# Block sums staged earlier, a branch result kept on chip and gates fetched a job ahead in a Fourier–Hyena encoder layer

## The chip, the cores and the metric

The kernel runs on one core of one Trainium2 chip. The metric is the device time of one execution in microseconds (us); the lower the better. All data are fp32. TensorE (PE) multiplies, VectorE (DVE), ScalarE (ACT) and GpSimd (POOL) do elementwise work, and transfers are issued from the queues of SyncE (SP) and GpSimd.

## The reference

Two sequences of 1024 rows and 1024 channels go through one encoder layer with two branches:

```
xn = rmsnorm(x, g_pre);  p = xn @ w_in        # columns: fv, fg, hv (3x), hg, mg (2x)
y_f = (fft2(fv).real * silu(fg)) @ w_fourier_out
v, x1, x2 = split(short_conv(hv))             # width-3 depthwise convolution
z = x1 * long_conv(v, k0);  z = x2 * long_conv(z, k1)
y_h = (z * silu(hg)) @ w_hyena_out
g_f, g_h = split(sigmoid(mg + b_merge))
out = x + rmsnorm((g_f * y_f + g_h * y_h) @ w_out, g_post)
```

The long convolutions' filters come from a small network and are normalized. "F" below is g_f * y_f, "H" is g_h * y_h.

## The kernel before

Matrices are held transposed, channels on partitions, in tiles of 128 channels by 1024 positions. Precision is kept by splitting each fp32 operand into a high part (a cast on ACT, line 171) and a low part (a subtraction, line 181), and multiplying high·high, high·low and low·high. So a loaded tile must pass ACT and then DVE or GpSimd before PE can use it.

The program has four parts in order of time. First come the Fourier transforms of both sequences (`phase_fourier`). Then 16 filter spectra are made, with projections of w_in as PE's filler (`spill_gate`: a projection whose result goes to DRAM as `d_g`, optionally multiplied by the Fourier result `d_fz`). Then the convolutions (`branches`), 16 steps for sequence 0 and 16 for sequence 1, again with projections; their results go to `d_sh`. Twelve more projections of sequence 1 (`PLAIN`, tiles `wr`, `wh`, `wl`) fill the end of this part. The fourth part, `phase_blocks`, is where most of the edit lies.

`phase_blocks` runs 34 jobs. Each job makes two output tiles of 128 channels by 1024 positions as a 2x2 block product in seven instead of eight block multiplications (Strassen–Winograd). A job's weights (`prepare`, tile `wraw`, its block sums `wsum`) are prepared a job or two ahead. The right operand is shared by all jobs of a kind: four plain blocks (`room`, tiles `b`) and four block sums (`sum_of`, tiles `tl`/`th`). There are six operands. Operand 0 (x of sequence 1) serves ten "x" jobs, which make the rest of the projections; operands 1 to 4 serve four jobs each (F of sequence 0, H of 0, F of 1, H of 1); operand 5, the weight w_out, serves the last eight "o" jobs. Where the operand changes, here called a turn, 7 MB of new blocks and sums must be loaded and split while PE goes from one job to the next.

The block sums of operands 1 to 5 are computed in this same part by `staged` (lines 1027 to 1039): during jobs, SP loads four blocks into `draw`, GpSimd forms four sums into `dsum` with three instructions and writes them to `d_t`; for w_out it also copies the plain blocks to `d_wo`. There are 20 such calls of 1 MB in and 1 MB out.

Each job drains four 128x512 results (`out`, lines 1090 to 1122), in the order of (tile, half) (0,0), (1,1), (0,1), (1,0). PE's accumulators are read by ACT into `u` and `m` (`kept`, line 1080), and DVE combines a second accumulator with them into `gt` (three buffers). An x job then applies SiLU on ACT, multiplies by a factor `fz` loaded for this result, and stores to `d_g`. An F or H job loads the merge gate `fz` (line 1114), takes its sigmoid on ACT (line 1115) and multiplies on DVE. F is stored to `d_m` (line 1122); H is added onto it by an accumulating transfer from GpSimd's queue (line 1120). The loads of `fz` are issued where the result is drained.

The order on each engine is set by a scheduler that plays the program through its own timeline. `tc.issue_after` holds a piece back until an instruction has been placed. Memory pools that open later reuse the space of closed ones, and wait for those tiles.

Of the kernel before, what the change touches and what calls it, by code (L numbers as in the profile page):

```python
# [16 lines left out]
P = 128  # L17
D = 1024
# [143 lines left out]
class K:  # L162
# [34 lines left out]
    def setup(self, ctx):  # L197
        tc, nc, a = self.tc, self.nc, self.a
        self.cp = cp = ctx.enter_context(tc.tile_pool(name="cp", bufs=1))
        self.ps = ctx.enter_context(tc.tile_pool(name="ps", bufs=2, space=bass.MemoryType.PSUM))  # L200
        self.dr = ctx.enter_context(tc.tile_pool(name="dr", bufs=1, space=bass.MemoryType.DRAM))

        def ld(name, shape, src, eng=nc.sync):
            t = cp.tile(shape, F32, name=name)
            eng.dma_start(t, src)
            return t
        self.ident = ld("ident", [P, P], a["c_id"], nc.gpsimd)
        self.gpre = ld("gpre", [P, 8], a["g_pre"], nc.gpsimd)
# [20 lines left out]
        self.d_wo = [dt(f"d_wo{k}", [P, D]) for k in range(8)]  # L229
        self.d_sh = [[dt(f"d_sh{b}_{k}", [P, L]) for k in range(8)] for b in range(NB)]  # L230
# [559 lines left out]
    def conv_back(self, n, ct, B, ws):  # L790
# [3 lines left out]
        for g, pairs in GROUPS:  # L794
# [3 lines left out]
            nc.sync.dma_start(kt.rearrange("p a b -> p (a b)"), self.d_k[n][ct][:, o:o + 8 * P])  # L798
# [98 lines left out]

    def branches(self, nb, nct, ws):
# [10 lines left out]
        plain = list(self.PLAIN)  # L909
        Z, X = {}, {}  # L910
# [21 lines left out]
        for i, (b, n, c) in enumerate(steps):  # L932
# [33 lines left out]
    def phase_blocks(self):  # L966
# [6 lines left out]
        jobs = [("x", s, c) for c in range(0, 8, 2) for s in (0, 4, 5, 6) if (s, c) not in self.PLAIN]  # L973
        for q in range(4):
            jobs += [("fh"[q % 2], q // 2, c) for c in range(0, 8, 2)]
        jobs += [("o", u, t) for u in range(4) for t in (0, 2)]
# [3 lines left out]
        def source(q):  # L980
            d = (self.d_g[0][0], self.d_sh[0], self.d_g[1][0], self.d_g[1][4], self.d_wo)[q - 1]
            return lambda k: d[k]
        with ExitStack() as es:
# [5 lines left out]
            def prepare(i):  # L989
# [3 lines left out]
                for j in range(2):  # L993
                    out = r[:, 2 * j:2 * j + 2].rearrange("p a b -> p (a b)")
                    if kind == "o":
                        nc.gpsimd.dma_start(out.rearrange("p (k c) -> p k c", k=8), self.d_m[x][:, :, P * (c + j):P * (c + j) + P])
                    else:
                        nc.gpsimd.dma_start(out, a["w_in"][x, c + j] if kind == "x" else a[f"w_{kind}o"][c + j])
                s = gw.tile([P, 4, 512], F32, tag="sum", name="wsum", bufs=1)
# [9 lines left out]
                self.add(eng, s[:, 0:2], r[:, 2].unsqueeze(1).to_broadcast([P, 2, 512]), r[:, 3::-3])  # L1009
                self.add(eng, s[:, 2], s[:, 0], r[:, 0])  # L1010
                parts("s2", gw, ("s2h", "s2l"), s[:, 2], 1)
                h, l = [gw.tile([P, 2, 4, P], F32R, tag=t, name=t, bufs=1) for t in ("s13h", "s13l")]
                f = lambda t: t.rearrange("p s a b -> p s (a b)")
                self.split(f(h), f(l), s[:, 0:2], "dve", "act")
                A["s1"], A["s3"] = (h[:, 0], l[:, 0]), (h[:, 1], l[:, 1])
                self.add(eng, s[:, 3], s[:, 2], r[:, 1])
                parts("s4", gw, ("s4h", "s4l"), s[:, 3], 1)
# [9 lines left out]
            def staged(q, k):  # L1027

                src = source(q)
                r = ga.tile([P, 4, 512], F32, tag="draw", name="draw", bufs=1)  # L1030
                for i in range(2):
                    nc.sync.dma_start(f2(r[:, 2 * i:2 * i + 2]), src(k + 4 * i) if q < 5 else a["w_out"][(k + 4 * i) * P:(k + 4 * i + 1) * P])
                    if q == 5:
                        nc.gpsimd.dma_start(src(k + 4 * i), f2(r[:, 2 * i:2 * i + 2]))
                s = ga.tile([P, 4, 512], F32, tag="dsum", name="dsum", bufs=1)
                self.sub("pool", s[:, 0::2], r[:, 0:2], r[:, 1::2])
                self.sub("pool", s[:, 1], s[:, 2], r[:, 0])
                self.add("pool", s[:, 3], s[:, 1], r[:, 2])
                nc.gpsimd.dma_start(self.d_t[q][:, k], s)

            def room(q, i, n):

                out = []
                for k in range(4):
                    t = xp.tile([P, 2, 512], F32R, tag=f"x{'hl'[i - n]}{k + 4 * n}", name=f"b{i}{n}{k}", bufs=1)
                    nc.sync.dma_start(t[:, 1].bitcast(F32), source(q)(k + 4 * i)[:, 512 * n:512 * n + 512])
# [18 lines left out]
            for k in range(4):  # L1065
# [3 lines left out]
                s = (ga, gw)[k % 2].tile([P, 4, 512], F32, tag=("dsum", "sum")[k % 2], name="xsum", bufs=1)  # L1069
                self.sub("dve", s[:, 0::2], r[:, 0:2], r[:, 1::2])  # L1070
                self.sub("dve", s[:, 1], s[:, 2], r[:, 0])
                self.add("dve", s[:, 3], s[:, 1], r[:, 2])
                for j in (1, 2, 0, 3):
                    self.split(T[j][0][:, k], T[j][1][:, k], s[:, j], "dve", "act")
# [14 lines left out]

            def out(i, j, n, p, q, op):  # L1090
# [4 lines left out]
                c += j  # L1095
                s = slice(512 * n, 512 * n + 512)
                t = wp.tile([P, 512], F32, tag="gt", name="gt", bufs=3)
                f = None
                if kind != "x" or x in (0, 4):
                    f = gw.tile([P, 512], F32, tag="f", name="fz", bufs=3)  # L1100
                if kind == "x":
                    if f is not None:
                        nc.sync.dma_start(f, (self.d_sh if x else self.d_fz)[1][c][:, s])
                    if q is not None:
                        self.tt("dve", t, p, q, op)
# [6 lines left out]
                    return  # L1112
                h = kind == "h"
                nc.sync.dma_start(f, self.d_g[x][6 if h else 5][c][:, s])
                nc.scalar.activation(f, f, AF.Sigmoid, bias=self.bm[:, 8 * h + c:8 * h + c + 1])
                if q is not None:
                    self.tt("dve", t, p, q, op)
                self.mul("dve", t, p if q is None else t, f)
                if h:
                    nc.gpsimd.dma_start(self.d_m[2 * x + n][:, c], t, accum_op=ADD)  # L1120
                else:
                    nc.sync.dma_start(self.d_m[2 * x + n][:, c], t)

            pa, pb, m1 = first(A)
            for i, job in enumerate(jobs):
                end = i + 1 == len(jobs)
                turn = not end and operand[i + 1] != operand[i]
                q = operand[min(i + 1, len(jobs) - 1)]
                if operand[i] == 5 and operand[i - 1] != 5:
                    st.close()  # L1130
# [41 lines left out]
                for p, k in {1: (1, 0), 2: (1, 1), 3: (1, 2), 4: (1, 3), 5: (2, 0), 6: (2, 1), 7: (2, 2), 8: (2, 3)}.items() if i < nx else ():  # L1172
                    if p == i:
                        staged(*k)
                if nx <= i < nx + 12:
                    staged(3 + (i - nx) // 4, (i - nx) % 4)

    def open_rows(self, op, jobs):
        nc, a = self.nc, self.a
        self.op, self.jobs = op, jobs  # L1180
        self.gp = op.tile([P, D], F32, name="gp")
# [3 lines left out]
    def open_row(self, i):  # L1185
# [3 lines left out]
        row = [512 * half + P * (t + j) for j in range(2)]  # L1189
# [110 lines left out]
```

## Time and profile before

| | |
|---|---|
| median of 3 runs | 2526.48 us (2525.7 to 2534.88) |
| the profiled execution | 2530.01 us |
| span in the profile | 2528.2 us |
| PE busy | 2398.2 us, 95% |
| DVE busy | 2083.5 us, 82% |
| ACT busy | 1128.3 us, 45% |
| GpSimd busy | 695.8 us, 28% |
| mean granted TensorE clock | 0.981 |

Busy times are shares of the span from the first to the last instruction. "Idle before" names what ended an engine's wait. "Granted clock" is the share of full speed at which TensorE was allowed to run; a PE that is busy at half clock still counts as busy. The last part (`phase_blocks`) starts its first product at about 1765 us.

### The profile page before, as it was taken

How to read it: one execution, taken by the hardware profiler on the slowest of the kernel's cores; microseconds unless marked ns; L12 is line 12 of the kernel's file. 1: busy time of each engine (PE TensorE's matmuls, PEld its weight loads, DVE VectorE, ACT ScalarE, POOL GpSimd, SP SyncE). 2: the span in 40 equal slices, each digit the busy share in tenths (PEclk: the TensorE clock that was granted, in tenths of full speed). 3: DMA queues.
4: the chain of work that ended last, by engine and by line, in shares of the span. 5: the costliest groups of instructions: out<-in, count | busy, mean ns of one | idle time of the engine just before them, and what ended most of it. 6: DMA issues, size and time to landing. Idle time of an engine off the chain costs nothing.

```text
span 2528.2 us, 36972 instructions
## 1 busy us (share of the span) xinstructions
PE 2398.2 (95%) x13004; PEld 2069.9 (82%) x13004; DVE 2083.5 (82%) x3696; ACT 1128.3 (45%) x2068; POOL 695.8 (28%) x588
## 2 busy tenths in 40 slices
PE   6999999999989999999999999999897988899898
PEld 6998888888878888888888888887786777677786
DVE  7786788888788999998989999876666887766887
ACT  6546666666643333333222223323343544444543
POOL 0331222211233434430000001113443555424221
PEclk9999999999999999999999999999999999899999
DMA  7636555554555545545434444437677888967654
GB/s 267 203 106 219 196 168 159 162 165 152 175 179 179 184 158 174 160 150 200 142 126 140 136 142 137 144 112 245 232 283 253 298 309 273 314 224 201 196 175 134
DMA packets 228594, 478.65 MB, mean 189 GB/s; under 512 B 23526, under 2 KB 70855, under 8 KB 225464
## 3 DMA queue, kind: packets, MB, share of 16 engines
q1 hardware_dynamic: 198876, 365.85, 44.3%
q0 software_dynamic: 29344, 110.42, 13.0%
q8 instruction: 102, 1.67, 0.3%
q14 instruction: 84, 0.69, 0.1%
q10 hardware_dynamic: 188, 0.02, 0.0%
HBM read 308.42 MB, written 167.77 MB: 188 GB/s over the span
## 4 chain that ended last, share of the span: by engine, by line
PE 36%; DMA 8%; DVE 5%; issue 3%; ACT 2%; POOL 1%; SPq 0%; DVEq 0%; ACTq 0%; POOLq 0%
PE pg L194 14%; PE pin L194 14%; PE pT L194 4%; PE pX L194 4%; DMA fz<-d_g 2%; DMA tl<-d_t 2%; DVE gt L181 1%; DVE tl L181 1%; DMA draw<-d_sh 1%; DMA xraw<-d_x 1%; DMA d_g<-gt 1%; DMA wraw<-in_w_in 1%; PE tph L786 1%; DMA b<-d_g 1%; DVE b L181 1%
## 5 line engine op out<-in xcount | busy, mean ns | idle before, releaser
L194 PE MATMUL pin<-xh,wh 128*128 128x512 f32 x1472 | 578.2, 394 | 3.6 <-DVE v L177 1.8
L194 PE MATMUL pin<-xh,wl 128*128 128x512 f32 x1472 | 577.0, 393 | 2.5 <-POOL wl L181 2.5
L194 PE MATMUL pin<-xl,wh 128*128 128x512 f32 x1472 | 578.4, 393 | 0.0
L181 POOL TENSOR_TENSOR wl<-wr,wh 128x512 fp32r<-128x512 f32 x136 | 252.5, 1857 | 1158.9 <-ACT wh L171 1142.9
L194 PEld LDWEIGHTS pin<-xh,wh 128*128 128x128 f32 x1472 | 278.3, 189 | 54.9 <-DVE v L177 2.0
L194 PEld LDWEIGHTS pin<-xh,wl 128*128 128x128 f32 x1472 | 278.3, 189 | 54.4 <-POOL wl L181 3.8
L194 PEld LDWEIGHTS pin<-xl,wh 128*128 128x128 f32 x1472 | 278.6, 189 | 51.4 <-DVE xl L181 0.4
L194 PE MATMUL pT<-cinv,yh 128*128 128x256 f32 x1024 | 192.1, 282 | 0.0
L194 PEld LDWEIGHTS pT<-cinv,yh 128*128 128x128 f32 x1024 | 164.9, 190 | 9.4
L181 DVE TENSOR_TENSOR t<-pX,k 128x1024 f32<-128x1024 f32 x128 | 155.4, 1214 | 9.7 <-PE pX L194 8.7
L194 PE MATMUL pX<-bh,cfwd 128*128 128x256 f32 x768 | 160.1, 287 | 0.0
L194 PE MATMUL pg<-th,s13h 128*128 128x512 f32 x272 | 114.8, 422 | 43.2 <-ACT u L1080 38.7
L171 ACT CAST wh<-wr 128x512 fp32r<-128x512 f32 x136 | 83.8, 616 | 148.2 <-PE pin L194 103.2
L171 ACT CAST yh<-y 128x512 fp32r<-128x512 f32 x128 | 79.4, 621 | 152.3 <-DVE y L181 119.6
L194 PE MATMUL pT<-cinv,yl 128*128 128x256 f32 x512 | 144.9, 283 | 1.2 <-DVE yl L181 1.2
L171 ACT CAST bh<-b 128x512 fp32r<-128x512 f32 x144 | 88.7, 618 | 121.3 <-DVE b L181 82.0
L181 DVE TENSOR_TENSOR bl<-b,bh 128x512 fp32r<-128x512 f32 x144 | 111.0, 772 | 23.7 <-ACT bh L171 23.6
L194 PEld LDWEIGHTS pX<-bh,cfwd 128*128 128x128 f32 x768 | 125.5, 191 | 2.9
L194 PE MATMUL pg<-tl,s13h 128*128 128x512 f32 x272 | 114.3, 420 | 13.7 <-DVE tl L181 13.7
L194 PE MATMUL pg<-b,wh 128*128 128x512 f32 x384 | 119.6, 391 | 1.0 <-DVE b L181 1.0
L181 DVE TENSOR_TENSOR gt<-gt,fz 128x512 f32<-128x512 f32 x96 | 106.0, 1110 | 9.9 <-ACT gt L771 5.6
L194 PE MATMUL pg<-th,s13l 128*128 128x512 f32 x272 | 112.6, 414 | 0.0
(309 smaller groups left out, 5806.2 us busy)
## 6 DMA issues: line engine op xcount, KB each, us to landing
k<-d_k SPq DMA_DIRECT2D x128, 512.0 KB, 4.0
wr<-in_w_in SPq DMA_DIRECT2D x136, 256.0 KB, 3.2
d_g<-gt SPq DMA_DIRECT2D x124, 256.0 KB, 3.3
d_t<-dsum POOLq DMA_DIRECT2D x20, 1024.0 KB, 9.9
tl<-d_t SPq DMA_DIRECT2D x20, 1024.0 KB, 12.0
d_k<-kt SPq DMA_DIRECT2D x128, 128.0 KB, 2.2
d_k<-kt SPq DMA_DIRECT2D x64, 256.0 KB, 2.4
fz<-d_g SPq DMA_DIRECT2D x64, 256.0 KB, 5.9
```

Source lines behind the costliest of these rows:

```text
L171: self.rounded = nc.scalar.copy(h, src)
L181: return e.tensor_tensor(out, a, b, op=op)
L194: return self.nc.tensor.matmul(out, lhsT, rhs, start=start, stop=stop, skip_group_check=shared)
L786: nc.tensor.transpose(tp[:, q * P:(q + 1) * P], eo[:, e, q], self.ident)
```

## The change

1. The sums of operands 1, 2 and 5 (F and H of sequence 0, and w_out) are no longer staged during the jobs but in the convolution steps of sequence 1: 24 half-size calls, one or two a step, each 512 KB in, four GpSimd instructions on 128x256 in place (`fold`), 512 KB out; `issue_after` keeps each behind the load of a step's last filter spectrum.
2. The sums of operands 3 and 4 come from the x jobs' own results. x jobs of the kinds 0 and 4 now pair tiles c and c+4; their four results go into one tile `res` (two buffers), which is stored as before and then folded in place by GpSimd and written to `d_t`. The loads of these blocks go away.
3. F stays in SBUF (`yf`, eight tiles of 1024 positions); H is added to it by GpSimd, and one store from SP writes the sum. The accumulating transfers and F's own stores go away.
4. `fz` is fetched a job ahead: after each drained result SP loads the factor for the same result of the next job (four buffers instead of three).
5. Weight sums are made in place in `wraw` by four 128x512 additions instead of one of 128x1024 and two of 128x512; the sums of x likewise.
6. At each turn the low parts of one of the four sums (j = 0) and of one of the three plain blocks' groups that are loaded (n = 1) move from DVE to GpSimd.

```diff
+    def fold(self, eng, r):
+        self.sub(eng, r[3], r[1], r[3])
+        self.sub(eng, r[1], r[0], r[1])
+        self.sub(eng, r[0], r[3], r[0])
+        self.add(eng, r[2], r[0], r[2])
+    def staged(self, q, k, half):
+        r = self.wp.tile([P, 4, 256], F32, tag="draw", name="draw", bufs=1)
+        s = slice(256 * half, 256 * half + 256)
+        for i in range(2):
+            src = {1: self.d_g[0][0], 2: self.d_sh[0]}[q][k + 4 * i] if q < 5 else a["w_out"][(k + 4 * i) * P:(k + 4 * i + 1) * P]
+            nc.sync.dma_start(r[:, 2 * i:2 * i + 2], src.rearrange("p (n c) -> p n c", n=2)[:, :, s])
+        if q == 5:
+            nc.gpsimd.dma_start(self.d_wo[:, k, :, s], r)
+        self.fold("pool", [r[:, j] for j in range(4)])
+        nc.gpsimd.dma_start(self.d_t[q][:, k, :, s], r)
...
+            if b == 1:
+                for _ in range(1 + (i % 2)):
+                    if stage:
+                        with tc.issue_after(self.spectrum.ins):
+                            self.staged(*stage.pop(0))
...
-                    self.split(h, l, l.bitcast(F32), "dve", "act")
+                    self.split(h, l, l.bitcast(F32), "pool" if n else "dve", "act")
...
-                nc.sync.dma_start(l.bitcast(F32), self.d_t[q][:, :, j])
-                self.split(h, l, l.bitcast(F32), "dve", "act")
+                nc.sync.dma_start(l.bitcast(F32), self.d_t[q][:, :, self.SLOT[j]])
+                self.split(h, l, l.bitcast(F32), "pool" if j == 0 else "dve", "act")
...
+                if kind == "x" and f is not None:
+                    if i not in R:
+                        R[i] = ga.tile([P, 4, 512], F32, tag="res", name="res", bufs=2)
+                    t = R[i][:, 2 * j + n]
+                elif kind == "f":
+                    if (x, c) not in Y:
+                        Y[x, c] = (xp if c < 4 else yf).tile([P, L], F32, tag=f"xl{4 + c}" if c < 4 else f"y{c}", name="yf", bufs=1)
+                    t = Y[x, c][:, s]
...
+                    if f is not None and (j, n) == (1, 0):
+                        r = R.pop(i)
+                        self.fold("pool", [r[:, m] for m in range(4)])
+                        nc.gpsimd.dma_start(self.d_t[3 + (x == 4)][:, jobs[i][2][0]], r)
...
-                if h:
-                    nc.gpsimd.dma_start(self.d_m[2 * x + n][:, c], t, accum_op=ADD)
...
+                    if h:
+                        y = Y[x, c][:, s]
+                        self.add("pool", y, y, t)
+                        nc.sync.dma_start(self.d_m[2 * x + n][:, c], y)
+                fetch(i + 1, j, n)
```

PE's order of products inside `phase_blocks` is the same in both kernels. The order around them moves at these places.

On SP, in the jobs of F of sequence 0 before the first turn into H: `fz` are the gates (d_g_5 those of F, d_g_6 those of H), `draw` the blocks to be staged, `b` and `tl` the next operand. Before:

```order
L1114 DMA fz<-d_g_5_4_144 128x512
L1122 DMA d_m_236<-gt 128x512
L1114 DMA fz<-d_g_5_5_145 128x512
L1046 DMA b_21622<-d_sh_0_253 128x512
L1046 DMA b_21624<-d_sh_1_254 128x512
L1046 DMA b_21626<-d_sh_2_255 128x512
L1046 DMA b_21628<-d_sh_3_256 128x512
L1032 DMA draw<-in_w_out 128x1024
L1046 DMA b_21638<-d_sh_4_257 128x512
L1122 DMA d_m_237<-gt 128x512
L1114 DMA fz<-d_g_5_6_146 128x512
```

The same place now:

```order
L1119 DMA fz<-d_g_5_4_144 128x512
L1119 DMA fz<-d_g_5_5_145 128x512
L1119 DMA fz<-d_g_5_6_146 128x512
L1063 DMA b_21750<-d_sh_0_246 128x512
L1063 DMA b_21752<-d_sh_1_247 128x512
L1063 DMA b_21754<-d_sh_2_248 128x512
L1063 DMA b_21756<-d_sh_3_249 128x512
L1063 DMA b_21766<-d_sh_4_250 128x512
L1119 DMA fz<-d_g_5_7_147 128x512
```

F's stores and the staging loads have gone from between the gates and the operand's blocks, and a gate stands one job further ahead of its use.

On GpSimd at the turn into H of sequence 0 (`wsum` weight sums, `dsum` staged sums, `d_m` the accumulating transfers). Before:

```order
L181 TENSOR_TENSOR wsum<-wraw 128x1024
L181 TENSOR_TENSOR wsum<-wsum,wraw 128x512
L998 DMA wraw<-in_w_ho 128x1024 x2
L181 TENSOR_TENSOR wsum<-wsum,wraw 128x512
L1120 DMA d_m_236<-gt 128x512
L1120 DMA d_m_237<-gt 128x512
L1034 DMA d_wo_246<-draw 128x1024
L1034 DMA d_wo_250<-draw 128x1024
L181 TENSOR_TENSOR dsum<-draw 128x2x512
```

The same place now:

```order
L181 TENSOR_TENSOR wraw<-wraw 128x512
L181 TENSOR_TENSOR yf<-yf,gt 128x512
L181 TENSOR_TENSOR wraw<-wsum,wraw 128x512
L181 TENSOR_TENSOR tl_21840<-tl_21840,th_21839 128x2048
L181 TENSOR_TENSOR b_21937<-b_21937 128x512
L181 TENSOR_TENSOR b_21939<-b_21939 128x512
L1028 DMA wraw<-in_w_ho 128x1024 x2
L181 TENSOR_TENSOR b_21941<-b_21941 128x512
L181 TENSOR_TENSOR b_21943<-b_21943 128x512
L181 TENSOR_TENSOR yf<-yf,gt 128x512
```

GpSimd has no staging here any more; it has the splits of the next operand and the additions of H, one behind the other.

On SP at the end of the Fourier part (`hidr`, `w` and `dec` feed the first filter, `cfw` and `xl` the other work after the Fourier part). Before:

```order
L730 DMA wr<-in_w_in 128x512 x4
L871 DMA hidr<-d_h 128x1024
L613 DMA w_2993<-in_filt_w 64x256
L614 DMA w_2993<-in_filt_w 64x256
L619 DMA dec<-in_filt_decay 128x256
L638 DMA db<-in_hyena_d 128x128
L878 DMA cfw_3087<-in_c_fw 128x512
```

Now the load of `hidr` stands 18 rows further down:

```order
L730 DMA wr<-in_w_in 128x512
L773 DMA d_g_0_0_124<-gt 128x512
L871 DMA hidr<-d_h 128x1024
L613 DMA w_2986<-in_filt_w 64x256
L614 DMA w_2986<-in_filt_w 64x256
L619 DMA dec<-in_filt_decay 128x256
```

Ahead of it stand all eight loads of `xl` and the loads and stores of the first projections. The first filter begins later, behind the first projections.

More of the change, by code (lines that the diff above doesn't have):

```diff
@@ L909, in branches @@
         plain = list(self.PLAIN)
+        stage = [(q, k, h) for q in (1, 2, 5) for k in range(4) for h in range(2)]
         Z, X = {}, {}
@@ L1025, in halves @@
                 return [(t[0][:, k], t[1][:, k]) for k in range(4)]
[L1027 to L1039, printed above, removed]
             def room(q, i, n):
@@ L1068, in phase_blocks @@
                     nc.sync.dma_start(f2(r[:, 2 * i:2 * i + 2]), self.d_x[1][k + 4 * i])
[L1069 to L1072, printed above, removed]
+                self.fold("dve", [r[:, j] for j in range(4)])
                 for j in (1, 2, 0, 3):
-                    self.split(T[j][0][:, k], T[j][1][:, k], s[:, j], "dve", "act")
+                    self.split(T[j][0][:, k], T[j][1][:, k], r[:, self.SLOT[j]], "dve", "act")
             for j in range(4):
@@ L1088, in first, with fetch @@
                 return pa, pb, m1
+            G, R, Y = {}, {}, {}
+            def fetch(i, j, n):
+                if i >= len(jobs):
+                    return
+                kind, x, c = jobs[i]
+                if kind == "o" or (kind == "x" and x not in (0, 4)):
+                    return
+                f = gw.tile([P, 512], F32, tag="f", name="fz", bufs=4)
+                s = slice(512 * n, 512 * n + 512)
+                if kind == "x":
+                    src = (self.d_sh if x else self.d_fz)[1][c[j]]
+                else:
+                    src = self.d_g[x][5 + (kind == "h")][c[j]]
+                nc.sync.dma_start(f, src[:, s])
+                G[i, j, n] = f
             def out(i, j, n, p, q, op):
@@ L1188, in open_row @@
         b, half = u // 2, u % 2
-        row = [512 * half + P * (t + j) for j in range(2)]
+        row = [512 * half + P * t[j] for j in range(2)]
         o, x = [], []
```

87 lines of the change are left out of this document (44 added, 43 removed).

## The prediction

> **What bounds the kernel now.** I read the page first, then the engines' busy time by stage, PE's waits, the chain of waits, and single groups.
>
> ```profile
> span 2528.2 us, 36972 instructions
> PE 2398.2 (95%) x13004; PEld 2069.9 (82%) x13004; DVE 2083.5 (82%) x3696; ACT 1128.3 (45%) x2068; POOL 695.8 (28%) x588
> ```
>
> PE is busy for 95% of the span, so 130 us is all that an edit without fewer products can win, apart from slow-clock time. Where it lies is read from the stages (length, then busy us of PE, PEld, DVE, ACT, POOL, then clock, DMA share, GB/s):
>
> ```profile
> 216.00:705.00 489.00, 478.31 (x2560) 411.91 (x2560) 398.58 (x917) 315.27 (x680) 114.52 (x80) 0.99 0.53 173
> 705.00:1200.00 495.00, 487.40 (x2847) 430.38 (x2845) 467.68 (x821) 181.91 (x306) 169.45 (x149) 0.99 0.53 174
> 1200.00:1600.00 400.00, 400.00 (x2433) 357.47 (x2432) 371.09 (x686) 118.80 (x201) 9.26 (x5) 1.00 0.43 137
> 1760.00:1940.00 180.00, 170.15 (x736) 139.43 (x737) 119.16 (x131) 65.58 (x109) 72.50 (x57) 0.98 0.74 263
> 1940.00:2060.00 120.00, 97.05 (x394) 77.55 (x393) 85.91 (x76) 55.30 (x82) 60.05 (x43) 0.91 0.78 279
> 2060.00:2140.00 80.00, 71.89 (x297) 57.10 (x295) 66.47 (x59) 38.91 (x56) 42.70 (x38) 0.96 0.90 300
> 2140.00:2220.00 80.00, 67.83 (x263) 53.64 (x262) 58.13 (x56) 38.09 (x55) 43.66 (x38) 0.89 0.94 308
> 2220.00:2300.00 80.00, 71.92 (x300) 57.96 (x299) 60.98 (x65) 43.76 (x65) 25.52 (x19) 0.96 0.69 224
> 2300.00:2380.00 80.00, 70.16 (x285) 55.62 (x284) 54.20 (x65) 39.49 (x59) 28.31 (x28) 0.94 0.81 219
> 2380.00:2520.00 140.00, 138.52 (x612) 114.38 (x610) 115.81 (x216) 58.95 (x123) 28.59 (x25) 1.00 0.46 145
> ```
>
> The convolutions of sequence 1 (1200 to 1600) leave PE no gap. The blocks from 1760 to 2520 do: length less busy sums to 72.5 us, and length times missing clock (0.02 of 180, 0.09 of 120, and so on) to 34.4 us. Together 107 us are lost there, nearly all between 1940 and 2380, with the five turns and the jobs of F and H. Whom PE waits for there:
>
> ```profile
> PE pg L194 <- ACT u L1080: 38.7, 11, 11.5
> PE pg L194 <- DVE tl L181: 18.8, 10, 3.6
> PE pg L194 <- ACT m L1080: 7.3, 5, 2.5
> PE pg L194 <- ACT th L171: 4.6, 4, 3.0
> PE pg L194 <- DVE b L181: 1.0, 2, 0.7
> ```
>
> The copies `u` and `m` of accumulators (46.0 us) and the splits of the next operand (24.4 us). The copies are short; ACT is late for them because it stands at a sigmoid whose gate has not landed, or because DVE stands at a `gt` whose store has not ended. The chain around the longest wait, and the waits by engine between 1760 and 2380:
>
> ```profile
> 1934.91 0.69 DVE gt L181
> 1935.79 9.73 DMA fz<-d_g
> ...
> 1946.90 0.72 ACT fz L1115
> ...
> 1952.11 0.49 ACT u L1080
> 1952.64 20.53 PE pg L194 x82
> ```
>
> ```profile
> SPq L1114 <- DVE gt L181: 117.5, 28, 11.6
> ACT fz L1115 <- DMA fz<-d_g: 73.5, 30, 7.2
> ACT th L171 <- DMA tl<-d_t: 36.1, 12, 5.7
> DVE gt L181 <- DMA d_g<-gt: 18.6, 7, 7.6
> ```
>
> The gate's load starts when DVE has finished with an earlier `gt`, so the load's 9.73 us stand on the path. Not all of u's waits are of this kind. Five, together 13.8 us, come just behind a turn, where DVE is still splitting blocks; the first and the last:
>
> ```profile
> 1996.77 0.49 PE L194 MATMUL pg<-th,s13h 128*128 128x512 f32 x1 [2.60 <-ACT u L1080]
> 2371.76 0.49 PE L194 MATMUL pg<-th,s13h 128*128 128x512 f32 x1 [1.73 <-ACT u L1080]
> ```
>
> So gates and stores hold 46.0 - 13.8 = 32.2 us of waits, the turns 24.4 + 13.8 = 38.2. Shared out in this proportion, the lost clock adds 15.7 and 18.7: 48 us for gates and stores, 57 for turns.
>
> The Trainium skill ("TensorE: Matmul & The Clock Gate", What's actually happening) says that the clock halves after an idle window of about 3.4 us. The trace is harsher: 0.91 to 0.96 of clock is granted in stages where hardly a wait is that long. By the page's rule, the waits of 2 to 3 us that I leave at turns would cost no clock, and the sum would be some 10 us lower.
>
> **The change, part by part.**
>
> Gates a job ahead, and F and H without transfers on the way. A job holds 84 products; at the pace of the last stage (138.52 us for 612, 0.226 each) it lasts 19 us, twice the 9.73 us of the slowest gate. The four loads of a job still go through SP in order, so a late store could hold them; I leave 4 us of the 48 for that and for H's additions, which now wait on GpSimd before DVE gets a `gt` back.
>
> The x jobs lose the wait for `gt` stores but get one for `res`. Its cycle:
>
> ```profile
> d_g<-gt SPq DMA_DIRECT2D x124, 256.0 KB, 3.3
> d_t<-dsum POOLq DMA_DIRECT2D x20, 1024.0 KB, 9.9
> L181 POOL TENSOR_TENSOR dsum<-dsum,draw 128x512 f32<-128x512 f32 x40 | 63.7, 1592 | 2.2
> L181 POOL TENSOR_TENSOR dsum<-draw 128x1024 f32<-128x1024 f32 x20 | 51.5, 2574 | 107.9 <-DMA d_t<-dsum 53.4 <-DMA draw<-d_sh 35.6 <-DMA draw<-d_g 11.5
> ```
>
> Store 3.3, four folds of 1.59, write 9.9: 19.6 us after the job's last result, and the buffer is wanted about one job (19 us) after it. Between 0 and, if the write takes twice its median, 10 us for each of four pairs of jobs; I take 4 in all. Left of the 48: 8. Gain 40.
>
> The turns. Before, staging with its loads and writes runs beside the first three turns, at a DMA share of 0.78 to 0.94; it has ended before the last two (2220 to 2380, where GpSimd's busy time is down to 25 to 28 us of 80). Those two stages lose 8.1 + 9.8 us of waits and 3.2 + 4.8 of clock, 25.9; taking out the gates' 48/105 leaves 14, or 7 a turn. I price all five at 7: 35 instead of 57. Against that stand the splits that move to GpSimd:
>
> ```profile
> L181 DVE TENSOR_TENSOR tl<-tl,th 128x2048 fp32r<-128x2048 f32 x20 | 52.9, 2647 | 28.4 <-ACT th L171 28.4
> L181 DVE TENSOR_TENSOR b<-b 128x512 fp32r<-128x512 f32 x60 | 53.1, 924 | 0.6 <-ACT b L171 0.5
> L181 POOL TENSOR_TENSOR wl<-wr,wh 128x512 fp32r<-128x512 f32 x136 | 252.5, 1857 | 1158.9 <-ACT wh L171 1142.9
> ```
>
> GpSimd takes 1.86 for what DVE does in 0.92, and for 2048 elements, from 1.59 and 2.57, about 1.6 + 3 x 0.98 = 4.5, with the fp32r output 5.3, against 2.65. The sum j = 0 is the third product of the job, so 2.6 us more are exposed at worst, while DVE is rid of 6.3 us a turn. Bounds for five turns: -10 to +13; I take +8. Gain 57 - 35 - 8 = 14.
>
> The Trainium skill ("GPSIMD Engine Reference", Engine selection) advises against this step: elementwise work of two inputs belongs on VectorE, as GpSimd is about twice as slow. The trace agrees (1.86 to 0.92). It also says that the two share SBUF interfaces.
>
> Staging in the convolutions of sequence 1. It adds 96 GpSimd instructions on 128x256, 48 loads on SP and 32 writes on GpSimd's queue. PE is full there and DVE 93% busy, so what matters is DVE. The same instruction with GpSimd 34% busy (705 to 1200) and idle (1200 to 1600), then two neighbours in the blocks with and without GpSimd at work, and the nearest GpSimd row:
>
> ```profile
> L181 DVE TENSOR_TENSOR y<-t 128x512 f32<-128x512 f32 x59 | 45.8, 777 | 0.4
> L181 DVE TENSOR_TENSOR y<-t 128x512 f32<-128x512 f32 x55 | 37.5, 681 | 0.2
> 1842.89 1.77 DVE L181 TENSOR_TENSOR gt<-gt,fz 128x512 f32<-128x512 f32 x1
> 1845.19 0.68 DVE L181 TENSOR_TENSOR gt<-gt,fz 128x512 f32<-128x512 f32 x1
> L181 POOL TENSOR_TENSOR wor<-wfv 128x256 f32<-128x256 f32 x16 | 13.0, 819 | 6.4 <-DVE wo L181 3.5 <-DMA wfv<-in_w_fv 2.4 <-DVE x L181 0.4
> ```
>
> 96 x 0.82 = 79 us of GpSimd. If DVE lost 1.09 of each 1.77 us beside it, that would be 49 us, against DVE's 29 us of idle time in 400, or 39 over the whole stretch of some 540: 10 us on the end. At the rate of the first sequence (14% slower at 34%), it is 79 x 0.14 / 0.34 = 33 us at most, inside the slack. Bounds 0 to 10 for DVE, and a few for projections whose `wl` queue behind a fold at the end; I take 3.
>
> The filters. Their first product moves 160 rows down PE's order, the last stays. PE has other work meanwhile, and DVE is busy for 82% of that stage, so the delay can be caught up. Bounds 0 to 0.226 x 160 = 36; I take 1. In-place weight sums: 4 x 1.59 = 6.4 us on GpSimd instead of 2.57 + 2 x 1.59 = 5.8, prepared a job ahead: nothing.
>
> **Sum.** Against the profiled execution (2530.0; its span 2528.2): -40 - 14 + 3 + 1 = -50, so 2480. The median of the runs is 3.5 lower, so 2476.5; I say 2477.
>
> **Rivals.**
>
> Turns cleared (0.18): without staging the 7 MB of a turn land in time, and only the start of each turn is lost, 2 us each. For it: the last stage runs at clock 1.00 with 1.5 us lost. Against: the last two turns wait without staging too. Turns 10 plus gates 8 leave 18 of 105: gain 87, less 4: 2444.
>
> DVE bound in sequence 1's convolutions (0.14): DVE's two-input instructions slow to 1.77 beside each fold, and late filters do not catch up; 10 + 15 us more: 2502.
>
> Gates still late (0.10): the change does not do what it says, since SP issues in order and 117.5 us of its waits before gate loads were for DVE. H's stores now wait for GpSimd ahead of them. The 48 stay, 14 - 4 remain: 2516.
>
> GpSimd takes DVE's place at the turns (0.10, slower): its queue holds, in order, 5.3 + 4 x 1.86 = 12.7 us of splits and 8 x 1.6 = 12.8 us of weight sums and H additions, 25.5 us in a job of 19. If PE waits for what exceeds DVE's old 6.3 us, that is 19 a turn and 96 in all, of which 8 are counted: up to 2565; I name 2550. It decides from 10 us a turn. Against: weights are made a job ahead, and only j = 0 and n = 1 come from GpSimd.
>
> **How the numbers follow.** The forecast has 0.48, with 2460 to 2495 as its own range. From 2438 (some two fifths of the first rival lie below, 0.07) to 2522 (the last and a fifth of the one before lie above, 0.12) holds 8 in 10. Half a per cent (12.6 us) is what this measurement can tell from no change. Below 2513.9 lie the forecast, the first two rivals and a third of the fourth case: 0.83; same 0.08; slower 0.09.
>
> **What would show it.** ACT's waits for `fz` near nothing instead of 73.5, and PE's for `u` under 15. PE's waits between the first product and the last stage at 25 to 35 instead of 71, the rest at the turns, on `tl`, `th` and `b`, some ended by POOL. DVE's `y` at 0.70 to 0.75 in sequence 1 with PE above 99% there. I am wrong if PE waits for POOL by more than 20 us, or if PE's first product of the blocks starts later than 1775.

## The result, and the profile after

The changed kernel takes 2559.6 us (median of 4 runs, 2557.5 to 2563.3) against 2529.6 for the kernel before beside it: 1.0119 of its time [1.0093, 1.0144], 30 us slower. The prediction was 2477 us and faster. The profiled execution took 2563.32 us; its page begins:

```profile
span 2561.5 us, 37092 instructions
PE 2402.7 (94%) x13004; PEld 2070.6 (81%) x13004; DVE 2085.8 (81%) x3693; ACT 1126.4 (44%) x2065; POOL 834.1 (33%) x709
```

PE and DVE do what they did; the 33 us are waits and slow clock. To place them, both traces are cut at the same products of PE: the filter stage (first projection to first transform), the convolutions of sequence 1 with the step to the blocks, and the blocks (first to last block product). First before, then after (length, then busy us of PE, PEld, DVE, ACT, POOL, then clock, DMA share, GB/s):

```profile
215.90:740.40 524.50, 507.85 (x2699) 436.60 (x2698) 427.80 (x978) 327.63 (x705) 122.74 (x89) 0.98 0.53 172
1246.40:1764.90 518.50, 516.75 (x3011) 456.26 (x3009) 448.08 (x795) 160.54 (x274) 53.75 (x32) 1.00 0.45 147
1764.90:2518.60 753.70, 682.86 (x2857) 551.83 (x2855) 558.92 (x660) 338.80 (x545) 301.15 (x244) 0.95 0.74 244
```

```profile
215.60:755.00 539.40, 509.81 (x2690) 435.45 (x2689) 427.41 (x980) 327.22 (x708) 125.82 (x89) 0.97 0.52 170
1261.80:1814.90 553.10, 531.48 (x3026) 465.58 (x3025) 457.43 (x791) 157.26 (x269) 162.77 (x154) 0.98 0.57 187
1814.90:2552.10 737.20, 674.78 (x2857) 548.43 (x2856) 547.77 (x664) 345.88 (x554) 332.49 (x243) 0.96 0.57 189
```

The filter stage lost 14.9 us and the convolutions 34.6; the blocks gained 16.5, where the prediction had 54. PE's waits in the second and the third stretch of after:

```profile
PE pin L194 <- POOL wl L181: 13.6, 3, 7.9
PE pin L194 <- DMA wh<-d_w: 7.6, 2, 4.2
...
PE pg L194 <- ACT u L1094: 32.5, 9, 8.0
PE pg L194 <- ACT m L1094: 14.4, 7, 4.0
PE pg L194 <- POOL tl L181: 13.1, 3, 6.8
```

`u` and `m` are waited for as long as before (46.9 us, before 46.0), and ACT still stands at gates. Its largest wait in the blocks, and the first gate of F, on ACT and where DVE multiplies by it:

```profile
ACT fz L1155 <- DMA fz<-d_g: 119.4, 45, 9.5
...
1967.35 1.28 ACT L1155 ACT_TABLE_LOAD   x1 [5.87 <-DMA fz<-d_g]
1968.64 0.72 ACT L1155 ACTIVATE fz<-fz,bm 128x512 f32<-128x512 f32 x1
...
2021.74 1.29 DVE L181 TENSOR_TENSOR yf<-yf,fz 128x512 f32<-128x512 f32 x1
```

ACT stands 5.87 us for a gate that nobody wants for another 53. Here PE had other work. Later the same kind of wait reaches PE (the gate at 2170.71 is multiplied by at 2192.02):

```profile
2170.71 0.72 ACT L1155 ACTIVATE fz<-fz,bm 128x512 f32<-128x512 f32 x1 [9.53 <-DMA fz<-d_g]
2174.42 0.58 ACT L1094 COPY m<-pg 128x512 f32<-128x512 f32 x1
2175.05 0.79 PE L194 MATMUL pg<-b,s4h 128*128 128x512 f32 x1 [3.98 <-ACT m L1094]
```

The load was moved a job ahead, and the scheduler moved the sigmoid with it. ACT takes its instructions in order in all these rows, so a gate that lands late holds up `u` and `m` however early it was fetched. By the order on ACT a sigmoid stood 0.9 copies of accumulators ahead of its own result before, on average, and 2.7 now; a job has three such copies.

Nine of PE's sixteen waits for `u` and `m`, 28.0 of the 46.9 us, come right after ACT stood at a gate. The longest, 8.01 us, does not. A split that the change gave to GpSimd runs there, and an addition on DVE beside it, 0.68 us long elsewhere, takes 4.38:

```profile
2397.91 4.94 POOL L181 TENSOR_TENSOR tl<-tl,th 128x2048 fp32r<-128x2048 f32 x1
2399.02 4.38 DVE L181 TENSOR_TENSOR wsum<-wraw 128x512 f32<-128x512 f32 x1
2404.67 0.79 PE L194 MATMUL pg<-th,s13h 128*128 128x512 f32 x1 [8.01 <-ACT u L1094]
```

ACT's next instruction waits for that `wsum`, and `u` stands behind it.

### The profile page after: what moved, and what is told of

It reads as the page before. It is cut to its first block, busy times and chain, and to the rows that moved or that the text cites. A ratio compares the mean times of both kernels' runs of the same rounds, so it can differ in the third digit from the quotient of the medians.

```text
span 2561.5 us, 37092 instructions
## 1 busy us (share of the span) xinstructions
PE 2402.7 (94%) x13004; PEld 2070.6 (81%) x13004; DVE 2085.8 (81%) x3693; ACT 1126.4 (44%) x2065; POOL 834.1 (33%) x709
## 5 line engine op out<-in xcount | busy, mean ns | idle before, releaser
L181 POOL TENSOR_TENSOR wl<-wr,wh 128x512 fp32r<-128x512 f32 x136 | 234.5, 1725 | 692.7 <-ACT wh L171 650.5
L181 POOL TENSOR_TENSOR draw<-draw 128x256 f32<-128x256 f32 x96 | 103.1, 1074 | 348.4 <-DMA draw<-d_g 209.3
L181 DVE TENSOR_TENSOR s13l<-wraw,s13h 128x1024 fp32r<-128x1024 f32 x34 | 43.3, 1272 | 103.4 <-ACT s13h L171 103.3
```

The lines of the kernel that those rows point to most:

```text
L181: return e.tensor_tensor(out, a, b, op=op)
```

## Experiments

Every run is timed in five rounds beside the kernel before (medians 2524 to 2527 us). "Stages" are the three stretches above in the run's own trace: filters, convolutions with the step, blocks; before 524.5 / 518.5 / 753.7, after 539.4 / 553.1 / 737.2. Where runs share a part of the program, their traces still differ by up to 6 us in the filters and 9 in the convolutions, so smaller differences there say nothing.

### The filters: 4 KB of address

e1_shift, from before:

```diff
+            mf.tile([P, D], F32, name="pad")
```

> The kernel before, with one unused tile of 4 KB per partition in the first pool of the filter stage, so that this stage's and the convolutions' tiles lie 4 KB further on; nothing else. Theory A (addresses): the filters' network output moves onto tiles of the Fourier part that come free later, so the scheduler places the first filter behind projections; expected: the first filter product at about 300 us instead of 276, the last at 755 instead of 740, time 15 us above before (2540 to 2550), the blocks as before. Rival B: the filters come late in the changed kernel for other reasons, or the delay is caught up; expected: time within 5 us of before.

Measured: 1.0083 [1.0065, 1.0101], +21 us, of which 15 lie in the filters; stages 539.5 / 522.6 / 748.3.

e2_ownpool, from after:

```diff
-        r = self.wp.tile([P, 4, 256], F32, tag="draw", name="draw", bufs=1)
+        r = self.sp.tile([P, 4, 256], F32, tag="draw", name="draw", bufs=1)   # sp: opened behind mi
```

(The tile for g_post in the last part, which shared the staging tile's place, moves to the last part's pool.)

> The changed kernel with the staging tile taken from a pool of its own that lies behind the others, so that no other tile of filters and convolutions moves. Theory A: first filter product back at 276, last at 740; time 15 us below the changed kernel, 1.005 to 1.007 of before (2541 to 2547). The 27 us lost in sequence 1's convolutions stay. Rival B: time as the changed kernel, 1.012 of before.

Measured: 1.0052 [1.0035, 1.0070]; stages 521.0 / 550.1 / 736.2. The first filter product of after, then of e1_shift:

```profile
L194 PE MATMUL pXf<-b,cfw x128: 270/275/555, 299.9 to 739.7; 128*128 128x128 f32 x128
```

```profile
L194 PE MATMUL pXf<-b,cfw x128: 270/275/552, 300.0 to 739.9; 128*128 128x128 f32 x128
```

An unused tile of 4 KB makes the whole delay; without it the first filter product stands at 277.6. Which old tile the scheduler waits for there was not singled out.

### The sigmoids held, and the turn's splits

e3_sigmoid, from e2_ownpool (`copied` is the last `u` or `m`):

```diff
-                    nc.scalar.activation(f, f, AF.Sigmoid, ...)
+                    with tc.issue_after(self.copied.ins):
+                        nc.scalar.activation(f, f, AF.Sigmoid, ...)
```

> As e2_ownpool, and each gate's sigmoid is held on ACT behind the copy of accumulators (u or m) that stands ahead of its own result, instead of standing a job early right behind the fetch. Theory S (ACT still waits for the gate's landing, only a job earlier): ACT's waits for fz fall from 119 us to under 20, PE's waits for u and m in the blocks from 47 to 20 to 30, time 15 to 25 us below e2_ownpool. Rival G (the blocks wait for GpSimd, whose queue in an H job holds more than a job): ACT's waits fall, but PE's waits only change their name; time within 5 us of e2_ownpool.

Measured: 0.9885 [0.9861, 0.9909], 48 us below e2_ownpool; stages 518.5 / 546.6 / 692.1. ACT has no wait for a gate left, and PE's two largest in the blocks are:

```profile
PE pg L194 <- ACT u L1094: 20.5, 8, 6.6
PE pg L194 <- POOL tl L181: 6.9, 2, 4.3
```

Two lines that move no work turn the change from slower to faster. PE's order is the same in both. A small part of the gain has another name: early sigmoids stand between the SiLUs of x jobs, and ACT loads its function table five times in the blocks of e2_ownpool, 1.28 us each, once in those of e3_sigmoid.

e4_turn, from e2_ownpool, and e6_sig_turn, both edits:

```diff
-                    self.split(h, l, l.bitcast(F32), "pool" if n else "dve", "act")
+                    self.split(h, l, l.bitcast(F32), "dve", "act")
...
-                self.split(h, l, l.bitcast(F32), "pool" if j == 0 else "dve", "act")
+                self.split(h, l, l.bitcast(F32), "dve", "act")
```

> As e2_ownpool, and the splits that the change moved to GpSimd at the turns (one sum of four, one group of plain blocks) are back on DVE. Theory G: PE's 13 us of waits for POOL at the turns vanish, and so do gates that stand behind H's stores, which wait for GpSimd; time 10 to 20 us below e2_ownpool. Theory S: DVE's splits of 2.65 and 0.92 us take their place, PE's waits for u stay; time within 6 us of e2_ownpool.

> e3_sigmoid and e4_turn together. If both causes are independent: e3's 48 us and e4's 11 us below e2_ownpool, 2478 to 2486. If the sigmoids' hold has already uncovered the turns' splits (PE waits for POOL's tl fell from 13.5 to 6.9 us there): 4 to 7 us below e3_sigmoid, 2486 to 2490.

Measured: e4_turn 1.0012 [0.9998, 1.0026], stages 521.2 / 541.2 / 726.4; e6_sig_turn 0.984 [0.9822, 0.9858], stages 521.5 / 540.9 / 682.9. The splits on GpSimd cost the blocks 9.8 us without the hold and 9.2 with it, as two separate costs would. The times are 11 and 7 us apart, and e6_sig_turn's 2486.9 us lies in the range of the other expectation, so whether the two add up in full is not settled.

### What the hold needs

e5_before_sig is before with the same hold on its sigmoids.

> The kernel before, with the same hold on the sigmoids as in e3_sigmoid and nothing else: loads of gates are issued where they were, each sigmoid stands behind the copy of accumulators ahead of its result. Theory S (in the kernel before, too, ACT waited for gates whose results were not due yet; three buffers already let the loads run three results ahead): ACT's waits for fz fall from 73.5 us to under 15, time 25 to 45 us below before. Rival L (the load itself is late, as the prediction read it, and only fetching it earlier helps): the wait moves to the sigmoid's new place, time within 10 us of before.

Measured: 0.9954 [0.9938, 0.9969], only 10 us; blocks 740.1. ACT's waits for gates fall from 73.5 to 16.1 us, so theory S is right on the wait and wrong on its price: PE still waits 35.7 us for `u`, now with DVE late, which waits 16.6 us for stores of `gt` to end. The gates lay over something else. Two runs leave staging out:

```diff
-                        staged(*k)
...
-                    staged(3 + (i - nx) // 4, (i - nx) % 4)
...
-                nc.sync.dma_start(l.bitcast(F32), self.d_t[q][:, :, j])
+                nc.sync.dma_start(l.bitcast(F32), <a tile of d_k of the same shape>)
```

> The kernel before without staging: no blocks loaded, added or written back in the jobs; the sums of operands 1 to 5 are loaded at the same places in the same size from data that has nothing to do with them, and w_out's plain blocks from another tensor. Sigmoids as before, no hold. Theory T (the turns' loads and staging in the jobs cost the 57 us of the prediction's split on their own): the blocks fall from 754 to 690 to 710, time 40 to 60 us below before. Theory M (a late sigmoid and late operands lie over each other; whichever is left sets PE's waits): 10 to 30 us below before.

> As e13_nostage, with the sigmoids held as in e5_before_sig, which alone took 14 us from the blocks of before. Theory M: both together take clearly more than the two alone, 55 to 75 us below before, as in e6_sig_turn's blocks (683 against 754). Theory T: the hold adds its 10 to 14 us to e13_nostage and no more. If the blocks stay above 715, other parts of the change (results folded on chip, sums in place, F kept) carry the rest.

Measured: e13_nostage 0.9833 [0.9814, 0.9852], e14_nostage_sig 0.9734 [0.9717, 0.9751]. Their blocks, without and with the hold:

```profile
1766.40:2476.70 710.30, 669.41 (x2857) 544.39 (x2855) 498.38 (x658) 338.87 (x545) 179.16 (x160) 0.98 0.62 193
```

```profile
1763.00:2449.30 686.30, 659.37 (x2857) 539.34 (x2855) 499.19 (x659) 336.49 (x544) 178.70 (x160) 0.99 0.63 200
```

Taking staging out of the jobs is worth 43 us alone, the hold 14 alone and 24 behind it, both 67. So no other part of the change is needed for its gain in the blocks. Staging's loads and its additions went together in these runs. Staging also slowed DVE: without it DVE is busy for 498.4 us in the blocks instead of 558.9, with 658 instructions instead of 660. How the 43 us divide between loads, waits and a slower DVE is not known.

What the rest of the change does in the blocks, four more runs say. e16_turn_dram and e12_dram send F and H through DRAM again, from e4_turn and e6_sig_turn:

```diff
-                        self.add("pool", y, y, t)
-                        nc.sync.dma_start(self.d_m[2 * x + n][:, c], y)
+                        nc.gpsimd.dma_start(self.d_m[2 * x + n][:, c], t, accum_op=ADD)
+                    else:
+                        nc.sync.dma_start(self.d_m[2 * x + n][:, c], t)
```

> As e4_turn (no hold on the sigmoids, the turn's splits on DVE), with F and H through DRAM as before the change. e4's blocks took 726, those of e13_nostage 710. If the difference is H: its stores stand in SP's queue behind GpSimd's additions, and the gates' loads behind the stores, so that early sigmoids wait longer: blocks 708 to 716, time 10 to 18 us below e4_turn (2530 with before at 2525). If not: within 5 us of e4_turn.

> As e6_sig_turn, with F stored to DRAM and H added to it by an accumulating transfer from GpSimd's queue, as before the change: 32 stores more, 32 additions of 1.7 us on GpSimd less. If DVE waits for a gt whose store has not ended once the sigmoids are out of the way (16.6 us in e5_before_sig's trace): 8 to 15 us above e6_sig_turn. If GpSimd's additions cost what the stores cost: within 5 us of it.

Measured: e16_turn_dram 0.9938 [0.9919, 0.9958], 21 us below e4_turn, blocks 705.3; e12_dram 0.9827 [0.9805, 0.9849], blocks 679.6, the same time as e6_sig_turn. The chain of waits of after, and SP's queue at the same place, show one way in which this costs time while gates are taken early:

```profile
2158.56 3.50 POOL wraw L181 x2
2162.06 1.71 POOL yf L181
2164.68 8.07 DMA fz<-d_g
...
2163.78 0.32 SPq L1160 DMA_DIRECT2D d_m<-yf  x1
2164.21 0.87 SPq L1119 DMA_DIRECT2D fz<-d_g  x2
```

H's store waits on SP for GpSimd's addition, which stands behind weight sums, and the gates' loads stand behind the store. With the hold it costs nothing that can be measured. A second way was not separated: without GpSimd's additions of H, DVE is busy for 500.9 us in the blocks of e16_turn_dram instead of 532.9. With the hold as much DVE time goes (528.5 to 494.0) and the time stays, which speaks for the queue; without the hold no run tells them apart.

e17_turn_three and e11_three give the gates three buffers and loads at their own results again, from e4_turn and e6_sig_turn:

```diff
-                f = gw.tile([P, 512], F32, tag="f", name="fz", bufs=4)
+                f = gw.tile([P, 512], F32, tag="f", name="fz", bufs=3)
...
-                fetch(i + 1, j, n)
```

> As e4_turn, with the gates' loads written where the result is drained and three buffers, as before the change; F and H stay on chip. If the fourth buffer hurts a kernel without the hold, because the scheduler moves each sigmoid further ahead with its load: blocks 710 to 718, 8 to 16 us below e4_turn. If the lead does not matter there: within 5 us of e4_turn.

> As e6_sig_turn, with the gates' loads written where the result is drained and three buffers, as before the change. (With four buffers and the loads written there, SP's queue is that of e6_sig_turn but for nine neighbours that change places: the fetch a job ahead is one more buffer.) If the hold on the sigmoids brought the gain and a lead of three results is enough for a load of 3 to 10 us: within 6 us of e6_sig_turn, 0.982 to 0.987 of before. If the job's lead matters: ACT waits for fz by more than 20 us again, 10 to 25 us above e6_sig_turn.

Measured: e17_turn_three 0.9971 [0.9956, 0.9985], 12 us below e4_turn, blocks 716.1; e11_three 0.9873 [0.985, 0.9897], blocks 687.2. Fetched further ahead, the gates cost 10 us in the blocks without the hold (a sigmoid stands 1.7 copies ahead in e17_turn_three), with F and H on chip; with F and H through DRAM it was not tried. With the hold the difference (4 us in the blocks; the intervals touch) is not settled.

### The convolutions: queues and additions

The waits of after there have two forms. SP's next load into the one staging buffer waits for the write of the piece before, and weights stand behind it; and GpSimd waits for w_out's copy to leave the buffer before it adds in place, with a weight's split behind:

```profile
1301.59 1.19 SPq L914 DMA_DIRECT2D draw<-d_g  x2
1302.82 0.60 SPq L727 DMA_DIRECT2D wh<-d_w  x1
...
1308.18 0.79 PE L194 MATMUL pin<-xh,wh 128*128 128x512 f32 x1 [4.19 <-DMA wh<-d_w]
...
1663.83 0.77 POOL L916 DMA_DIRECT2D d_wo<-draw  x1 [7.85 <-DMA draw<-in_w_out]
1671.26 3.11 POOL L181 TENSOR_TENSOR draw<-draw 128x256 f32<-128x256 f32 x4 [6.67 <-DMA d_wo<-draw]
1674.33 1.26 POOL L181 TENSOR_TENSOR wl<-wr,wh 128x512 fp32r<-128x512 f32 x1
...
1675.65 0.80 PE L194 MATMUL pin<-xh,wl 128*128 128x512 f32 x1 [7.92 <-POOL wl L181]
```

All four runs go from e6_sig_turn (540.9 in this stage). e7_queues takes these waits away, e8_nofold the additions, e10_both both:

```diff
-        r = self.sp.tile([P, 4, 256], F32, tag="draw", name="draw", bufs=1)
+        r = self.sp.tile([P, 4, 256], F32, tag="draw", name="draw", bufs=2)   # e7, e10
...
-            nc.gpsimd.dma_start(self.d_wo[:, k, :, s], r)
+            <d_wo copied from w_out, DRAM to DRAM>                                # e7, e10
...
-        self.fold("pool", [r[:, j] for j in range(4)])                            # e8, e10
```

(The copies of w_out go out from GpSimd's queue behind an addition in e7_queues, from SP's queue in e10_both.)

> As e6_sig_turn, with the two waits taken away that stand in the queues in sequence 1's convolutions: two staging buffers instead of one, so that SP's load need not wait for the write of the piece before; and w_out is copied from DRAM to DRAM, so that GpSimd's first subtraction in place need not wait until the copy has left the buffer. Theory Q (the convolutions lose their 20 to 25 us because weights stand in SP's and GpSimd's queues behind staging): PE's waits there fall below 4 us, time 12 to 22 us below e6_sig_turn. Rival V (GpSimd's 96 additions slow VectorE down, which bounds that stage): PE's waits stay or change their name, time within 5 us of e6_sig_turn.

> As e6_sig_turn, without the additions of staging in the convolutions: the blocks are loaded and written back unchanged, so the operands 1, 2 and 5 get wrong sums; all transfers stay, and one staging buffer. Theory Q: SP's and GpSimd's queues still wait for the one buffer's transfers, so at least half of the loss stays: time within 8 us of e6_sig_turn. Rival V: with GpSimd's 100 us of additions gone, DVE is as fast as before in sequence 1 and the convolutions take their old 463 us: time 18 to 25 us below e6_sig_turn.

> e7_queues and e8_nofold together: two staging buffers, w_out copied from DRAM to DRAM (from SP's queue), and no additions in staging, so that operands 1, 2 and 5 get wrong sums; the transfers stay. If waits in queues (8.5 us in e7's trace) and additions (13.8 in e8's) make up the whole loss of 22 us in sequence 1's convolutions and the step to the blocks: these take 517 to 522 us, as before (518.5), time 2462 to 2468. If a third cost is left, such as the transfers themselves: 525 to 530 us, time above 2470.

Measured: 0.9797 [0.978, 0.9815], 0.9796 [0.9774, 0.9817] and 0.9732 [0.9709, 0.9755]; this stage took 532.4, 527.1 and 516.6 us. Each theory was to explain most of the 22 us; each explains about half (11 us of the time each, 27 together; 8.5, 13.8 and 24.3 in the traces), and together they are all of it. The halves rest on the times, since 8.5 us is within what traces of one program differ by here. e10_both's convolutions leave PE no gap, with all the transfers:

```profile
1244.00:1706.40 462.40, 462.36 (x2772) 411.69 (x2771) 411.51 (x749) 138.76 (x236) 49.30 (x40) 1.00 0.60 199
```

What the additions do to DVE is seen in e7_queues, where they meet no wait. DVE's groups in this stage of before, then of e7_queues:

```profile
L181 DVE TENSOR_TENSOR y<-t 128x512 f32<-128x512 f32 x62 | 42.9, 692 | 0.3
L181 DVE TENSOR_TENSOR yc<-q 128x512 f32<-128x512 f32 x32 | 20.5, 682 | 0.1
L181 DVE TENSOR_TENSOR b<-bs 128x256 f32<-128x256 f32 x30 | 11.2, 414 | 0.0
L181 DVE TENSOR_TENSOR t<-pX,k 128x1024 f32<-128x1024 f32 x62 | 75.4, 1216 | 6.3 <-PE pX L194 5.7
```

```profile
L181 DVE TENSOR_TENSOR y<-t 128x512 f32<-128x512 f32 x62 | 43.7, 704 | 0.3
L181 DVE TENSOR_TENSOR yc<-q 128x512 f32<-128x512 f32 x32 | 27.8, 909 | 0.1
L181 DVE TENSOR_TENSOR b<-bs 128x256 f32<-128x256 f32 x30 | 19.9, 703 | 0.0
L181 DVE TENSOR_TENSOR t<-pX,k 128x1024 f32<-128x1024 f32 x62 | 75.2, 1214 | 5.9 <-PE pX L194 5.3
```

`y`, which the prediction watched, is nearly as fast as ever, because the additions stand elsewhere: 14 of the 62 `y` ran beside one (0.79 us on average, the others 0.68), but 21 of the 32 `yc` (1.03) and 19 of the 30 `b` (0.87). DVE is busy for 43.6 us more than before in this stretch (452.5 against 408.9, without the step to the blocks). Its idle time fell from 53.7 to 25.0 us, which takes 29 of the 44; the other 15 made the stretch longer.

e9_wout_early, from e7_queues, stages w_out in the filter stage, with its copies from SP's queue:

```diff
+                if i % 2:
+                    with tc.issue_after(self.spectrum.ins):
+                        self.staged(5, i // 4, i // 2 % 2)
```

> As e7_queues, but the eight pieces of w_out, which depend on an input alone, are staged in the filter stage, one behind every second filter, where PE and DVE have gaps; in sequence 1's convolutions one piece a step is left, 16 instead of 24. If each addition of GpSimd in the full stage costs its share: e7 lost 14 us there (532 against 518 before), a third of it comes back, 4 to 5 us, and the filter stage takes it up: 2468 to 2474 with before at 2525. Rival: the filter stage is bounded by DVE at its end and pays the same back: 2474 to 2480.

Measured: 0.9826 [0.9805, 0.9847]; stages 540.8 / 523.4 / 683.7. The convolutions gain 9 us and the filter stage pays 20: the rival, and more. DVE is busy for 9.8 us more in the filters (436.4 against 426.7); what the queue of the copies adds was not tested.

### The best complete version

e15_q_dram is e7_queues and e12_dram.

> e7_queues and e12_dram together, a version that computes everything: two staging buffers, w_out copied from DRAM to DRAM, F and H through DRAM as before the change. If the two add up: 2470 to 2475 with before at 2525, the fastest of the complete versions. If F's stores collide with what e7_queues moved: 2476 to 2483.

Measured: 2469.5 us, 0.9772 [0.9754, 0.9790]: 57 us faster than before and, by the two ratios, some 88 faster than the change as made. Stages 520.9 / 531.2 / 678.7.

```profile
span 2464.9 us, 37174 instructions
PE 2380.4 (97%) x13004; PEld 2058.9 (84%) x13004; DVE 2050.2 (83%) x3718; ACT 1122.6 (46%) x2066; POOL 762.3 (31%) x692
```

## Why the prediction was wrong

**Gates a job ahead, F and H without transfers on the way: gain 40.** This step failed. It took the 9.73 us of a gate's load for a load issued too late. In fact the wait came too early. The sigmoid of that very chain, at 1946.90 in the kernel before, takes the first gate of F, and DVE multiplies by it 55.6 us later:

```profile
2002.51 1.76 DVE L181 TENSOR_TENSOR gt<-gt,fz 128x512 f32<-128x512 f32 x1
```

Fetching further ahead moved the wait with it: ACT's waits for `fz`, forecast near nothing, grew from 73.5 to 119.4 us. Instead of a gain of 40, the step's parts measured a loss in the blocks: the fetch with its fourth buffer 10 us (e17_turn_three), F and H on chip 21 (e16_turn_dram). Holding the sigmoids back, which the change did not do, is what gains: 44 us in the blocks of e2_ownpool (e3_sigmoid). The third rival (0.10) named the second part, H's stores in SP's queue, but no case had the blocks lose by the fetch itself.

The Trainium skill ("PSUM — Partial Sum Buffer", Engine vs sequencer instructions) says that the queues of ScalarE, VectorE and GpSimd are strictly first in, first out. The waits on ACT and GpSimd above agree, the 9.53 us at 2170.71 first: `m` stood behind it.

**The turns: 57 to 35, and +8 for the splits.** The split of the 107 us into 48 for gates and 57 for turns went wrong by charging waits to whoever ended them. Staging out of the jobs was worth 43 us (e13_nostage), not 22. Why the last two turns of before, which have no staging beside them, were too dear a measure was not tested. The +8 held as a number, 9.8 and 9.2, by luck in part: it priced slower splits, not the DVE instructions that a split on GpSimd holds up, such as the one of 4.38 us. The fourth rival (0.10) named a time near the measured one, 2550, by 19 us a turn; the splits cost 10 in all, so that nearness is luck too. The causes do not add: 14 and 43 alone, 67 together. From e13_nostage's 710.3 the steps lead to after: 705.3 with the change's other parts (e16_turn_dram), +21.1 for F and H, +9.8 for the splits: 736.2 in e2_ownpool, 737.2 in after.

**Staging in the convolutions: 3.** The measured loss is 22 to 35 us, by run. The extra DVE time was roughly right: 33 us forecast at most; without the step to the blocks DVE was busy for 408.9 us before, 430.6 in after, 434.4 in e6_sig_turn and 452.5 in e7_queues, 22 to 44 more. What failed is "inside the slack": of the 44 us, 29 went into idle time and 15 into the length of the stage, though 25 us of idle time were left. And the queues, "a few" in the prediction, were priced without the edit's own buffer, a single one whose next load waits for its last write on SP, ahead of weights.

**The filters: 1.** Measured 15. "Can be caught up" was false: between 640 and 756 us PE waits for DVE for 22.0 us (6.6 in the kernel before), so the stage has nothing to catch up with at its end. The bound of 36 held.

**Weight sums in place: nothing.** Not tried by itself; with the rest of the change's other parts it is inside the 5 us between e13_nostage and e16_turn_dram.

**What was to show it.** Two of the signs of being wrong came true: PE waits for POOL for 26.7 us in the last two stretches (20 was the limit), and the first product of the blocks starts at 1814.9 (1775). The range left this side out because two costs, bounded at 0 to 36 and 0 to 10, were taken near their lower ends, and because the gain of 40 had no bound on the side of a loss.

## What to carry to other kernels

When an engine waits for a load, look first for whom the load is: if the result is not due, the cure is to move the waiting instruction back, not the load forward. Where a scheduler places work by its own timeline, an earlier transfer pulls its consumer ahead with it, so tie the consumer to the work that it belongs to. In a stage that is full, the idle time of the second busiest engine or of a queue is only in part there to be used. Work that GpSimd takes over can hold up DVE instructions beside it. And a tile added to an early pool can move the order of everything behind it.

## What was not expected of the hardware

- GpSimd's additions slow only some of DVE's work. In e7_queues `yc<-q` and `b<-bs`, both inputs in SBUF, took 1.03 and 0.87 us on average beside an addition and 0.69 and 0.41 otherwise. The 13 `t<-pX,k` that ran beside one, with an input in PSUM, took 1.215 us, the other 49 1.213. The Trainium skill ("GPSIMD Engine Reference", Specifications) names DVE instructions with two SBUF inputs among those that contend; the rows agree.
- GpSimd pays as well: its 128x256 addition took 1.07 us on average in the changed kernel (96 of them, 103.1 us), against 0.82 for the row that the prediction priced it by.
- PE's 21.5 us of waits in the convolutions and the step came with 13.6 us of lost clock, though none was longer than 7.9 us: in a stage that was granted 1.00 before, the waits cost over half of themselves again.
